# Four-layer hybrid decoder step on one core: contiguous cache sums, a shift added in PSUM, and layer sums kept in DRAM

## The chip, the core and the metric
The kernel runs on one NeuronCore of a Trainium2 chip. The core has five engines that each work through a list of instructions of their own, in order: TensorE (PE) multiplies matrices into PSUM; VectorE (DVE), ScalarE (ACT) and GpSimd (POOL) do elementwise work; SyncE (SP) issues most of the DMA transfers, and GpSimd issues the gathers. An engine that waits for a semaphore holds up everything behind it in its list. The metric is the device time of one execution in microseconds.

## The reference, cut to what matters
A trunk of four layers (short gated convolution, sparse attention, RG-LRU, short gated convolution) runs over 1024 prompt tokens and 32 sample tokens, with 1024 features. Every layer ends with an out-projection and a layer norm of the sum with its input. The attention of the sample tokens reads a paged cache; of its key and value rows, weighted sums over blocks of 32 are made.

```python
def layer_norm(x, g, b):
    xf = x.astype(jnp.float32)
    mu = jnp.mean(xf, axis=-1, keepdims=True)
    var = jnp.mean(jnp.square(xf - mu), axis=-1, keepdims=True)
    return ((xf - mu) * lax.rsqrt(var + LN_EPS) * g.astype(jnp.float32) + b.astype(jnp.float32)).astype(x.dtype)
...
past = cache_nsa_kv[j][page_table].reshape(bs, n_pages * PAGE_SIZE, 4, N_KV, HEAD_DIM)
...
blocks = full[:, :n_cmp * CMP_BLOCK, :2].reshape(bsz, n_cmp, CMP_BLOCK, 2, N_KV, HEAD_DIM)
kv_c = jnp.einsum('bnjcgd,cjgd->bncgd', blocks, w_cmp)
...
return (jax.nn.silu(z) * b_gate * conv) @ w_out, new_buf     # a mixer's end: the out-projection
...
yp = layer_norm(ALPHA * yp + mp, ln_g[i], ln_b[i])
ys = layer_norm(ALPHA * ys + ms, ln_g[i], ln_b[i])
```

## The kernel before
**Layout.** Activations lie transposed: X is eight tiles of 128 features by 1056 tokens. Tokens are cut into three blocks j of 352. So that fp32 matrices can be multiplied in three passes of the faster fp32r type, every operand is held as two halves, a rounded high part and the rest (`split`: ScalarE writes the rounded copy, VectorE or GpSimd subtracts). One output tile of 128 features by 352 tokens is 24 products (8 feature tiles x 3 pairs of halves), accumulated in one PSUM bank; `dense` and `dense_steps` issue them.

**Order.** The first layer, parts of the attention's projections, the third and fourth layers and all out-projections are recorded and then ordered by a planner (`Rec`). It simulates the engines with the prices of `cost`, gives buffers out of rings, and at every moment starts on each engine the ready step with the earliest due number. The order that comes out is fixed; on the chip the engines only wait for each other. The prompt attention between them has a plan of its own with prices of its own.

**Layer A with the cache sums.** While layer A runs its 96 output tiles, `compress` is advanced by 0.7 steps per tile (`share`, RATE). Its 64 steps (8 groups jg of rows x 8 samples b) each gather 1 MB of cache pages into a `big` buffer (GpSimd's indirect DMA), write half of it back to DRAM (`raw`), multiply the other half (4 x 256 columns) by the weights, on VectorE for even b and on GpSimd for odd, and reduce the four rows to 256 columns on VectorE. From the second group on, GpSimd adds this to the running sum. The ring of `big` buffers also holds X and layer A's results U, so the gathers have fewer buffers the further layer A is.

**An out-projection (`out_phase`).** It is run after layers 1 to 3 (ln 0, 1, 2), in row blocks c of 128 features: c = 0 to 3 for all three j, then c = 4 to 7 for j = 0, for j = 1, for j = 2. Each (c, j) makes y = ALPHA x + projection. For ln 0, x is put together from X's halves on GpSimd; for ln 1 and 2 it is read from DRAM. From row block 0, a product with a matrix of ones gives a shift per token (`kt`); the shift is subtracted from every later y on GpSimd, and the result and its square are summed over c in `ss`, on VectorE or GpSimd by the table `SUMS`. The shifted y is split into X's two halves in place, but for the last two or three row blocks, which stay in a `ws` buffer (`late`). After c = 7 of a block j, `norm(j)` takes statistics by products with ones, computes some twenty small operations, broadcasts scale and offset by further products, and for each c puts the halves together again on GpSimd, multiplies, adds, applies gain and bias on ScalarE, writes the result to DRAM and splits it into X for the next layer.

The last layer ends in another function (`final_phase`), which the change does not touch. In ln 1 four of the output tiles are made by the attention and come in as `done`.

Of the kernel before, what the change touches and what calls it, by code (L numbers as in the profile page):

```python
# [13 lines left out]
ALU = mybir.AluOpType  # L14
# [226 lines left out]
class Rec:  # L241
# [27 lines left out]
    def cost(self, eng, name, a, k, out):  # L269
# [226 lines left out]
class Trunk:  # L496
# [16 lines left out]
    def setup(self):  # L513
# [4 lines left out]
        self.dp = self.pool("scratch", 1, space=DRAM)  # L518
        self.pre = {}
# [5 lines left out]
        self.ones_m = self.cp.tile([P, P], F32, name="ones_m")  # L525
        nc.vector.memset(self.ones_m, 1.0 / D)

# [100 lines left out]
    def dense_steps(self, ps, w, X, sl):  # L628
        n = 0
        for k in range(NCH):  # L630
            xh, xl = X[k][:, 0, sl], X[k][:, 1, sl]
            for a, b in ((w[:, 0, k], xh), (w[:, 0, k], xl), (w[:, 1, k], xh)):
                self.nc.tensor.matmul(ps, a, b, start=n == 0, stop=n == 23)  # L633
                n += 1
# [42 lines left out]
    def out_phase(self, pm, wsrc, U, X, ln, lp, res=None, done={}, spill=None, final=None, nxt=()):  # L677


        nc = self.nc  # L680
# [3 lines left out]
        kt = self.wx.tile([P, 1088], F32)[:, 0:T]  # L684
# [12 lines left out]
        def norm(j):  # L697
# [34 lines left out]
            for c in range(NCH):  # L732
                self.rec.shift = AHEAD[self.later]["norm"]
                d = late[c][:, sl] if c in late else self.ct(TC)
                xh, xl = X[c][:, 0, sl], X[c][:, 1, sl]
                if c not in late:
                    nc.gpsimd.tensor_add(d, xh.bitcast(F32), xl.bitcast(F32))
                    nc.vector.tensor_mul(d, d, RB[0])
                    (nc.gpsimd if c in NADD[ln][j] else nc.vector).tensor_add(d, d, RB[1])
                else:  # L740
                    nc.vector.tensor_mul(d, d, RB[0])
                    (nc.gpsimd if c in NADD[ln][j] else nc.vector).tensor_add(d, d, RB[1])
# [14 lines left out]
        for c, j in order:  # L757
# [3 lines left out]
            if (c, j) not in done:  # L761
                ps = self.mm(pm)[:, 0:TC]
                self.dense(ps, W[c], U, j)
            if j == 2 and c >= 4:
                self.fetch(nxt[c - 4:c - 3])
# [3 lines left out]
            xh, xl = X[c][:, 0, sl], X[c][:, 1, sl]  # L769
            x = self.ct(TC)  # L770
            if (c, j) not in done:
                if res is None:
                    nc.gpsimd.tensor_add(x, xh.bitcast(F32), xl.bitcast(F32))
                else:
                    nc.sync.dma_start(x, res[c][:, sl], rk=[("x", ln - 1, c, j)])
                stt(out=y, in0=x, scalar=ALPHA, in1=ps, op0=ALU.mult, op1=ALU.add)
            d = y
# [1635 lines left out]
```

## Time and profile before

| what | value |
|---|---|
| median of 3 runs | 2470.85 us (2468.2 to 2470.94) |
| profiled execution, its own time | 2474.15 us |
| its span from first to last instruction | 2472.4 us |
| mean granted TensorE clock | 0.967 |
| TensorE busy | 2326.4 us, 94% |
| VectorE busy | 1688.7 us, 68% |
| ScalarE busy | 1225.4 us, 50% |
| GpSimd busy | 1149.1 us, 46% |
| moved by DMA | 303 MB, 123 GB/s mean |

The stages by time: the X tiles are loaded and transposed until some 40 us; layer A with the cache sums runs to about 420 us; the out-projection ln 0 follows, then the attention's projections and the sample tokens' attention to about 930 us, the prompt attention to about 1470, ln 1 to about 1600, the RG-LRU layer to about 1840, ln 2 to about 1970, and the last layer to the end. A busy TensorE is not TensorE at its peak: products are pipelined, and a stretch at the low clock counts as busy too. So stretches are compared by the number of products in them as well as by the busy time. Since one helper records all planned operations, nearly all have line 307; tiles and shapes tell them apart.

### The profile page before, as it was taken

What the parts mean: (1) busy time and instruction counts of PE and PEld (TensorE: products, weight loads), DVE (VectorE), ACT (ScalarE), POOL (GpSimd) and SP (SyncE); (2) the same over time, 40 slices, a digit from 0 to 9 for tenths busy, and PEclk for the clock granted to TensorE, in tenths of its full rate; (3) what the DMA queues carried; (4) which work ended last, traced back from release to release, by engine and by line L of the source; (5) the groups of instructions that cost most, each with busy time, mean ns of one, the idle gap of its engine ahead of it and who ended that gap; (6) DMA issues with size and microseconds to landing.
All of it is one profiled execution on the core that took longest, in us unless ns stands there. A gap on an engine that the chain in (4) does not pass through costs nothing. (4 is left out here: it accounts for less than half of the span.)

```text
span 2472.4 us, 41243 instructions
## 1 busy us (share of the span) xinstructions
PE 2326.4 (94%) x14740; PEld 2252.1 (91%) x14740; DVE 1688.7 (68%) x3588; ACT 1225.4 (50%) x2809; POOL 1149.1 (46%) x1261
## 2 busy tenths in 40 slices
PE   8999899888989989999999999889999899999997
PEld 8999899877878879999999988889999899999996
DVE  5867776688358777777777777888877863334336
ACT  3111111234448778888888873467974342122123
POOL 3555575766137755565565554633464640000122
PEclk9999999988999989999999999989999899999998
DMA  8999998425456752111111323221112121211111
GB/s 278 327 296 336 280 295 274 129 84 204 125 173 224 243 195 56 35 46 43 44 50 46 97 91 98 71 81 52 56 48 78 39 59 45 59 35 46 49 45 71
DMA packets 320816, 303.01 MB, mean 123 GB/s; under 512 B 17926, under 2 KB 287718, under 8 KB 311140
## 3 DMA queue, kind: packets, MB, share of 16 engines
q1 hardware_dynamic: 311396, 233.28, 30.7%
q0 software_dynamic: 9216, 67.11, 7.8%
q8 instruction: 116, 1.90, 0.3%
q14 instruction: 88, 0.72, 0.1%
HBM read 228.66 MB, written 75.83 MB: 123 GB/s over the span
## 5 line engine op out<-in xcount | busy, mean ns | idle before, releaser
L307 PE MATMUL mm<-x,w 128*128 128x352 f32 x5760 | 955.3, 327 | 31.2 <-DVE c L307 14.6
L307 PEld LDWEIGHTS mm<-x,w 128*128 128x128 f32 x5760 | 943.2, 192 | 38.2 <-DVE c L307 16.7
L307 PE MATMUL mm<-big,w 128*128 128x352 f32 x2208 | 386.3, 334 | 9.1 <-DVE c L307 3.9
L307 PEld LDWEIGHTS mm<-big,w 128*128 128x128 f32 x2208 | 371.2, 196 | 12.6 <-DVE c L307 4.5
L307 POOL TENSOR_TENSOR w<-ws,w 128x1024 fp32r<-128x1024 f32 (+1 forms) x43 | 105.3, 2449 | 400.2 <-ACT w L307 378.6
L1959 DVE TENSOR_TENSOR c<-T,c 128x512 fp32r<-128x512 f32 (+1 forms) x320 | 204.8, 648 | 49.2 <-ACT c L1955 44.5
L1955 ACT CAST c<-T 128x512 fp32r<-128x512 f32 (+1 forms) x320 | 174.6, 552 | 57.9 <-PE T L1951 38.0
L307 ACT CAST w<-ws 128x1024 fp32r<-128x1024 f32 (+2 forms) x116 | 120.6, 1039 | 163.8 <-PE mm L307 123.2
L633 PE MATMUL D<-x,w 128*128 128x352 f32 x1008 | 195.4, 330 | 2.1 <-DVE big L2086 2.0
L1861 PE MATMUL A<-big 128*128 128x320 f32 (+11 forms) x832 | 182.2, 335 | 3.4 <-DVE ast L1886 1.6
L1966 PE MATMUL O<-c,big 128*128 128x256 f32 x1056 | 180.2, 291 | 0.5 <-ACT c L1955 0.2
L307 ACT CAST big<-aux 128x352 fp32r<-128x352 f32 (+3 forms) x116 | 45.2, 402 | 243.6 <-DVE aux L307 165.5
L633 PEld LDWEIGHTS D<-x,w 128*128 128x128 f32 x1008 | 159.9, 188 | 5.6 <-DVE big L2086 3.5
L307 DVE TENSOR_TENSOR w<-ws,w 128x1024 fp32r<-128x1024 f32 (+2 forms) x73 | 91.6, 1255 | 99.7 <-ACT w L307 98.9
L1966 PEld LDWEIGHTS O<-c,big 128*128 128x128 f32 x1056 | 147.0, 189 | 2.5 <-DVE c L1959 0.7
L1919 POOL TENSOR_SCALAR pr<-pr,G,ast 128x32 f32<-128x32 f32 (+6 forms) x192 | 126.4, 674 | 47.1 <-DVE ast L1930 42.3
L1861 PEld LDWEIGHTS A<-big 128*128 128x128 f32 x832 | 134.8, 193 | 10.2 <-PE A L1861 2.2
L307 DVE TENSOR_REDUCE csum<-big 128x256 f32<-128x1024 f32 x56 | 111.5, 1992 | 40.9 <-POOL big L307 40.6
L1915 ACT ACTIVATE pr<-pr,ast 128x32 f32<-128x32 f32 (+6 forms) x192 | 118.4, 619 | 18.1 <-DVE ast L1886 17.0
L307 ACT ACTIVATE aux<-ws,PT 128x352 f32<-128x352 f32 (+2 forms) x72 | 42.8, 594 | 163.8 <-DVE ws L307 161.8
L307 DVE SCALAR_TENSOR_TENSOR c<-c,mm 128x352 f32<-128x352 f32 x143 | 72.9, 514 | 73.2 <-ACT c L307 49.0
L307 POOL TENSOR_TENSOR big<-big,ws 128x1024 f32<-128x1024 f32 (+1 forms) x40 | 87.9, 2198 | 68.6 <-DMA ws<-in_b_w_cmp 49.7
(287 smaller groups left out, 4364.7 us busy)
## 6 DMA issues: line engine op xcount, KB each, us to landing
ws<-in_a_w_in SPq DMA_DIRECT2D x64, 512.0 KB
raw<-big SPq DMA_DIRECT2D x128, 256.0 KB
big<-raw SPq DMA_DIRECT2D x128, 256.0 KB
xs<-x SPq DMA_DIRECT2D x24, 352.0 KB
x<-xs SPq DMA_DIRECT2D x8, 1056.0 KB
ws<-in_a_w_out SPq DMA_DIRECT2D x16, 512.0 KB
ws<-in_c_w_in SPq DMA_DIRECT2D x16, 512.0 KB
big<-ud SPq DMA_DIRECT2D x21, 352.0 KB
```

The source lines that it names most:

```text
L307: getattr(real, name)(*[f(x) for x in a], **{q: f(x) for q, x in k.items()})
L633: self.nc.tensor.matmul(ps, a, b, start=n == 0, stop=n == 23)
L1861: nc.tensor.matmul(o, q[:, hl, i * P:(i + 1) * P], k, start=m == 0, stop=m == 1)
L1915: nc.scalar.activation(S[:, a:a + m], S[:, a:a + m], AF.Exp, bias=st[:, k:k + 1], scale=-1.0, accum_out=st[:, 3 + k:4 + k])
L1919: nc.gpsimd.tensor_scalar(S[:, a:a + m], S[:, a:a + m], G[:, i, 16 * k + h:16 * k + h + 1], st[:, 6 + k:7 + k], op0=ALU.mult, op1=ALU.mult)
L1955: nc.scalar.copy(x["H"][:, 0:n], x["tp"][:, 0:n])
L1959: nc.vector.tensor_sub(x["L"][:, 0:n], x["tp"][:, 0:n], x["H"][:, 0:n].bitcast(F32))
L1966: nc.tensor.matmul(O, v, M[:, y * P:(y + 2) * P], start=done[0] == 0, stop=done[0] == total - 1)
```

## The change
**Cache sums.** The reduction over four strided rows becomes three contiguous additions on VectorE in place in the gathered buffer: rows 0 and 1 plus rows 2 and 3 (512 columns), then the two halves of that (256), then that onto the running sum (256). GpSimd's addition and the buffer `csum` are gone.

**Out-projections.** The shift is no longer subtracted from y: a 25th product, of the ones matrix with the scaled negative shift, is added in PSUM for every row block but the first. For this the ones and `kt` are fp32r. For ln 0, x is no longer put together: two VectorE operations add the two halves of X to the PSUM tile, one after the other. The shifted sums are no longer split into X; they go whole to a DRAM scratch `dd` and are read back in `norm`, so GpSimd's addition of the halves there is gone as well. The late row blocks stay in their buffers as before. The read-back has a due number 3 later than the rest of the norm (`DAHEAD`).

**Planner.** A product of 352 columns is now priced at 162 ns instead of 149, which moves steps in every planned part. The tables of due shifts and of engine choices are the same.

```diff
-            return max(free(m) / 2.4 * (4 if m.dtype == F32 else 1), 107) + 2
+            return max(free(m) / 2.27 * (4 if m.dtype == F32 else 1), 50) + 7
...
+        self.dd = self.dp.tile([NCH, P, T], F32, name="dd")
...
-        self.ones_m = self.cp.tile([P, P], F32, name="ones_m")
+        ones = self.cp.tile([P, P], F32R, name="ones_m")
+        self.ones_m = ones.bitcast(F32)
         nc.vector.memset(self.ones_m, 1.0 / D)
+        self.ones_r = ones
...
-    def dense(self, ps, w, X, j):
+    def dense(self, ps, w, X, j, extra=None):
-        for _ in self.dense_steps(ps, w, X, slice(j * TC, (j + 1) * TC)):
+        for _ in self.dense_steps(ps, w, X, slice(j * TC, (j + 1) * TC), extra is None):
             pass
+        if extra is not None:
+            self.nc.tensor.matmul(ps, self.ones_r, extra, start=False, stop=True)
...
                 xh, xl = X[c][:, 0, sl], X[c][:, 1, sl]
-                if c not in late:
-                    nc.gpsimd.tensor_add(d, xh.bitcast(F32), xl.bitcast(F32))
+                if c in late:
+                    d = late[c][:, sl]
+                else:
+                    d = self.ct(TC)
+                    self.rec.shift += DAHEAD
+                    nc.sync.dma_start(d, self.dd[c][:, sl], rk=[("d", ln, c, j)])
+                    self.rec.shift -= DAHEAD
...
             if (c, j) not in done:
+                ps = self.mm(pm)[:, 0:TC]
+                self.dense(ps, W[c], U, j, k if c else None)
                 if res is None:
-                    nc.gpsimd.tensor_add(x, xh.bitcast(F32), xl.bitcast(F32))
+                    stt(out=ps, in0=xl, scalar=ALPHA, in1=ps, op0=ALU.mult, op1=ALU.add)
+                    stt(out=y, in0=xh, scalar=ALPHA, in1=ps, op0=ALU.mult, op1=ALU.add)
...
-                nc.scalar.activation(kt[:, sl], kp, AF.Copy, scale=float(NCH))
-                d = ss[:, 0, sl]
-                nc.vector.tensor_sub(d, y, kt[:, sl])
+                nc.scalar.activation(k, kp, AF.Copy, scale=-8.0 * NCH)
+            d = ss[:, 0, sl] if c == 0 else y
+            if c == 0 or (c, j) in done:
+                stt(out=d, in0=k.bitcast(F32), scalar=0.125, in1=y, op0=ALU.mult, op1=ALU.add)
...
-                nc.gpsimd.tensor_sub(d, y, kt[:, sl])
...
             if c not in late:
-                self.split(xh, xl, d, "act", "dve")
+                nc.sync.dma_start(self.dd[c][:, sl], d, wk=[("d", ln, c, j)])
...
-                v = g4[:, :, 0:256].rearrange("p j f -> p f j")
-                o = acc[:, b]
+                o, v = acc[:, b], g4[:, :, 0:256]
+                nc.vector.tensor_add(v[:, 0:2], v[:, 0:2], v[:, 2:4])
                 if jg == 0:
-                    nc.vector.tensor_reduce(out=o, in_=v, axis=AX.X, op=ALU.add, wk=[("sum", n)])
+                    nc.vector.tensor_add(o, v[:, 0], v[:, 1], wk=[("sum", n)])
                 else:
-                    t = rt.tile([P, 256], F32)
-                    nc.vector.tensor_reduce(out=t, in_=v, axis=AX.X, op=ALU.add, wk=[("sum", n)])
-                    nc.gpsimd.tensor_add(o, o, t)
+                    nc.vector.tensor_add(v[:, 0], v[:, 0], v[:, 1])
+                    nc.vector.tensor_add(o, o, v[:, 0], wk=[("sum", n)])
...
+DAHEAD = -3
```

Three places show how the order moves. The first is VectorE at the end of layer A, where `csum<-big` (before) and `big<-big` (after) are the last cache sums, `c<-mm,c` and `aux<-c,aux` make layer A's last results, and `big<-aux,big` splits them into U. Before:

```order
L307 TENSOR_REDUCE csum<-big 128x256
L307 SCALAR_TENSOR_TENSOR c<-mm,c 128x352
L307 TENSOR_TENSOR aux<-c,aux 128x352
L307 SCALAR_TENSOR_TENSOR c<-mm,c 128x352
L307 TENSOR_TENSOR aux<-c,aux 128x320
L307 TENSOR_REDUCE csum<-big 128x256
L307 TENSOR_TENSOR big<-big,ws 128x4x256
L307 TENSOR_REDUCE csum<-big 128x256
L307 TENSOR_TENSOR big<-aux,big 128x352 x2
L307 TENSOR_TENSOR big<-aux,big 128x320
```

VectorE at the same place after:

```order
L307 TENSOR_TENSOR big<-big 128x2x256
L307 SCALAR_TENSOR_TENSOR c<-c,mm 128x352
L307 TENSOR_TENSOR big<-big 128x256 x2
L307 SCALAR_TENSOR_TENSOR c<-mm,c 128x352
L307 TENSOR_TENSOR aux<-c,aux 128x352
L307 TENSOR_TENSOR big<-aux,big 128x352
```

The last sums of the cache now stand ahead of the last three results, and each result's split follows it directly. The second place is GpSimd at the start of the out-projection ln 0, where `c<-x` puts X's halves together, `c<-c,ws` subtracts the shift and `big<-big,c` adds to `ss`. Before:

```order
L307 TENSOR_TENSOR big<-big,ws 128x4x256
L307 TENSOR_TENSOR c<-x 128x352
L307 TENSOR_TENSOR big<-big,csum 128x256
L307 TENSOR_TENSOR c<-x 128x352 x2
L307 TENSOR_TENSOR c<-c,ws 128x352
L307 TENSOR_TENSOR big<-big,c 128x352
```

GpSimd at the same place after:

```order
L312 DMA big<-in_cache_nsa_kv,idx_447 128x2048
L307 TENSOR_TENSOR big<-big,ws 128x4x256
L307 TENSOR_TENSOR w<-ws,w 128x1024
L307 TENSOR_TENSOR big<-big,c 128x352 x7
L307 TENSOR_TENSOR w<-ws,w 128x1024
```

Of the three kinds of additions only those into `ss` are left. The third place is TensorE at the end of ln 0, where `mm<-big` and `mm<-big,w` are the last output tiles, `mm<-w,x` and `mm<-big,x` of 384 columns are the next layer's, and `aux<-ones_m,big` are the statistics of the last block. Before:

```order
L307 MATMUL mm<-big 128x352 x18
L307 MATMUL mm<-w,x 128x384 x54
L307 MATMUL mm<-big,x 128x384 x6
L307 MATMUL aux<-ones_m,big 128x1 x6
L307 MATMUL mm<-big,x 128x384 x6
```

TensorE at the same place after:

```order
L307 MATMUL mm<-big 128x352 x24
L307 MATMUL mm<-ws,ones_m 128x352
L307 MATMUL mm<-w,x 128x384 x24
L307 MATMUL aux<-ones_m,big 128x1 x6
L307 MATMUL mm<-w,x 128x384 x12
```

The statistics stand after 24 products of the next layer instead of 60, and a product of `ones_m` closes the tile.

## Rows read from the trace of the kernel before

**Rows 1.** The page: busy time by engine, and clock by fortieth of the span.
```profile
PE 2326.4 (94%) x14740; PEld 2252.1 (91%) x14740; DVE 1688.7 (68%) x3588; ACT 1225.4 (50%) x2809; POOL 1149.1 (46%) x1261
...
PEclk9999999988999989999999999989999899999998
```

**Rows 2.** Stretches: busy us of PE, PEld, DVE, ACT, POOL; clock, DMA share, GB/s.
```profile
100.00:150.00 50.00, 50.00 (x313) 50.00 (x313) 32.17 (x37) 8.03 (x14) 28.78 (x21) 1.00 0.93 303
150.00:420.00 270.00, 250.74 (x1502) 248.19 (x1501) 207.12 (x227) 48.89 (x90) 164.55 (x115) 0.97 0.93 296
420.00:480.00 60.00, 47.73 (x269) 46.01 (x269) 40.06 (x46) 14.12 (x28) 38.75 (x32) 0.89 0.58 181
480.00:630.00 150.00, 125.30 (x662) 115.03 (x661) 113.41 (x171) 58.14 (x116) 94.55 (x86) 0.89 0.40 133
1520.00:1655.00 135.00, 115.63 (x640) 111.54 (x639) 115.67 (x223) 62.30 (x121) 70.59 (x62) 0.89 0.24 76
1920.00:2010.00 90.00, 78.25 (x444) 76.09 (x443) 76.90 (x138) 41.25 (x81) 55.71 (x50) 0.89 0.15 41
```

**Rows 3.** Timeline of PE in layer A: start, us, operation, count [idle before, releaser].
```profile
272.01 44.08 PE L307 MATMUL mm<-x,w 128*128 128x352 f32 x264 [5.12 <-DVE c L307]
...
443.95 1.88 PE L307 MATMUL aux<-idf,SC 128*18 128x128 f32 x8 [9.47 <-DVE big L307]
...
450.13 1.94 PE L307 MATMUL aux<-c,ones_m 128*128 128x352 f32 x6
```

**Rows 4.** Timeline of all engines, around 266 us and around 440 us.
```profile
266.27 5.27 DVE L307 COPY ws<-PT 128x16 f32<-128x16 f32 x1
...
266.86 2.35 POOL L307 TENSOR_TENSOR big<-big,ws 128x1024 f32<-128x1024 f32 x1
269.15 2.34 POOL L307 TENSOR_TENSOR w<-ws,w 128x1024 fp32r<-128x1024 f32 x1
...
437.34 1.88 DVE L307 TENSOR_REDUCE csum<-big 128x256 f32<-128x1024 f32 x1 [4.11 <-POOL big L307]
...
442.88 1.14 ACT L307 CAST big<-aux 128x352 fp32r<-128x352 f32 x3 [33.86 <-DVE csum L307]
```

**Rows 5.** Groups by shape, 100 to 450 us: busy us, mean ns | idle before.
```profile
L307 DVE TENSOR_REDUCE csum<-big 128x256 f32<-128x1024 f32 x54 | 107.6, 1992 | 40.9 <-POOL big L307 40.6
L307 DVE TENSOR_TENSOR big<-big,ws 128x1024 f32<-128x1024 f32 x27 | 47.1, 1745 | 35.6 <-DMA raw<-big 12.0 <-DMA ws<-in_a_w_in 10.4 <-DMA ws<-in_b_w_cmp 6.3
...
L307 POOL TENSOR_TENSOR big<-big,csum 128x256 f32<-128x256 f32 x54 | 54.7, 1012 | 74.0 <-DVE csum L307 72.4 <-DMA raw<-big 1.6
```

**Rows 6.** The same view, 2010 to 2400 us, where GpSimd is nearly idle.
```profile
L307 DVE TENSOR_TENSOR w<-ws,w 128x1024 fp32r<-128x1024 f32 x29 | 35.5, 1226 | 93.6 <-ACT w L307 93.1
```

**Rows 7.** The same view, 480 to 630 us, of VectorE, GpSimd and ScalarE.
```profile
L307 DVE TENSOR_TENSOR c<-c 128x352 f32<-128x352 f32 x29 | 24.6, 872 | 4.5 <-ACT c L307 3.7 <-POOL c L307 0.8
L307 DVE TENSOR_TENSOR x<-c,x 128x352 fp32r<-128x352 f32 x23 | 21.6, 952 | 5.0 <-ACT x L307 5.0
L307 DVE TENSOR_TENSOR big<-big,c 128x352 f32<-128x352 f32 x21 | 18.2, 886 | 6.3 <-POOL c L307 4.8 <-ACT c L307 1.6
...
L307 DVE SCALAR_TENSOR_TENSOR c<-c,mm 128x352 f32<-128x352 f32 x10 | 5.1, 511 | 0.4 <-POOL c L307 0.4
...
L307 POOL TENSOR_TENSOR c<-x 128x352 f32<-128x352 f32 x32 | 36.9, 1173 | 6.5 <-DVE big L307 3.6 <-PE aux L307 2.9
...
L307 ACT ACTIVATE c<-c 128x352 f32<-128x352 f32 x10 | 5.0, 496 | 20.4 <-POOL c L307 20.4
```

**Rows 8.** Timeline of VectorE around 572 us, in the norm of ln 0.
```profile
571.78 0.52 DVE L307 TENSOR_TENSOR c<-c 128x352 f32<-128x352 f32 x1
...
573.40 1.26 DVE L307 TENSOR_TENSOR c<-c 128x352 f32<-128x352 f32 x1
```

**Rows 9.** Waits of PE, 480 to 630 us: total us, times, longest.
```profile
PE aux L307 <- POOL big L307: 8.3, 2, 4.4
```

**Rows 10.** The chain that ended last, in order of time: start, us, what.
```profile
1888.62 2.20 DMA c<-xc
```

More of the change, by code (lines that the diff above doesn't have):

```diff
@@ L621, in load_w, with dense_steps @@
         return w
-    def dense(self, ps, w, X, j):
-        for _ in self.dense_steps(ps, w, X, slice(j * TC, (j + 1) * TC)):
-            pass
-    def dense_steps(self, ps, w, X, sl):
+    def dense(self, ps, w, X, j, extra=None):
+        for _ in self.dense_steps(ps, w, X, slice(j * TC, (j + 1) * TC), extra is None):
+            pass
+        if extra is not None:
+            self.nc.tensor.matmul(ps, self.ones_r, extra, start=False, stop=True)
+    def dense_steps(self, ps, w, X, sl, last=True):
         n = 0
@@ L632, in dense_steps @@
             for a, b in ((w[:, 0, k], xh), (w[:, 0, k], xl), (w[:, 1, k], xh)):
-                self.nc.tensor.matmul(ps, a, b, start=n == 0, stop=n == 23)
+                self.nc.tensor.matmul(ps, a, b, start=n == 0, stop=n == 23 and last)
                 n += 1
@@ L683, in out_phase @@
         ss = ss[:, 0:2 * T].rearrange("p (a n) -> p a n", a=2)
-        kt = self.wx.tile([P, 1088], F32)[:, 0:T]
+        kt = self.wx.tile([P, 1088], F32R)[:, 0:T]
         stat = lp.tile([P, 3, 24], F32, name="stat")
@@ L760, in out_phase @@
             sl = slice(j * TC, (j + 1) * TC)
[L761 to L765, printed above, removed]
+            xh, xl = X[c][:, 0, sl].bitcast(F32), X[c][:, 1, sl].bitcast(F32)
+            k = kt[:, sl]
             if j == 0 and NCH - c <= self.nws - 2 and c >= 4:
@@ L768, in out_phase @@
             y = done[c, j] if (c, j) in done else late[c][:, sl] if c in late else self.ct(TC)
-            xh, xl = X[c][:, 0, sl], X[c][:, 1, sl]
             x = self.ct(TC)
             if (c, j) not in done:
+                ps = self.mm(pm)[:, 0:TC]
+                self.dense(ps, W[c], U, j, k if c else None)
                 if res is None:
-                    nc.gpsimd.tensor_add(x, xh.bitcast(F32), xl.bitcast(F32))
+                    stt(out=ps, in0=xl, scalar=ALPHA, in1=ps, op0=ALU.mult, op1=ALU.add)
+                    stt(out=y, in0=xh, scalar=ALPHA, in1=ps, op0=ALU.mult, op1=ALU.add)
                 else:
                     nc.sync.dma_start(x, res[c][:, sl], rk=[("x", ln - 1, c, j)])
-                stt(out=y, in0=x, scalar=ALPHA, in1=ps, op0=ALU.mult, op1=ALU.add)
-            d = y
+                    stt(out=y, in0=x, scalar=ALPHA, in1=ps, op0=ALU.mult, op1=ALU.add)
+            if j == 2 and c >= 4:
+                self.fetch(nxt[c - 4:c - 3])
             if c == 0:
```

9 lines of the change are left out of this document (3 added, 6 removed).

## The prediction
> **What bounds the kernel now.** I read the page's first part and its clock line first, then a table of stretches, then the timeline and the groups of instructions inside the stretches where TensorE is not full. TensorE is busy for 94% of the span, and the clock line shows 9 or 8 tenths in nearly every slice [rows 1]: this is a kernel of one engine, and only what TensorE does, waits for, or does at the low clock counts. The stretch from 100 to 150 us shows it unhindered: 313 products of 352 columns in 50 us at clock 1.00, so 0.160 us for each [rows 2].
>
> In five stretches it is hindered. I call lost the idle time of PE plus (1 - granted clock) x stretch; the clock has two levels, 1.2 and 2.4 GHz, so a mean of 0.89 is some 22% of the stretch at the lower one, each time after a wait. By [rows 2]: layer A with the cache sums, 150 to 420, 270 - 250.7 + 0.03 x 270 = 27.4 us; its end, 420 to 480, 12.3 + 6.6 = 18.9; the first out-projection's norm and the next layer's start, 480 to 630, 24.7 + 16.5 = 41.2; the second out-projection, 1520 to 1655, 19.4 + 14.9 = 34.2; the third, 1920 to 2010, 11.8 + 9.9 = 21.7. Together 143 us. The change touches what runs in all five, and adds TensorE work; so the question is how much of the 143 comes back.
>
> **What ends the waits.** In layer A, PE waits 5.12 us before 272.0 and 9.47 us before 444.0, both for VectorE [rows 3]. The first is a VectorE copy of 16 columns that took 5.27 us: it lies over a GpSimd multiplication of 2.35 us and a GpSimd subtraction of 2.34 us that follow each other [rows 4]. The second is in-order blocking: VectorE stood 4.11 us at a cache reduction whose input GpSimd was still multiplying, and ScalarE's rounding of layer A's last U waited 33.9 us, up to 442.9, for such a reduction, because that U's buffer is one that a gathered page held [rows 4]. In the out-projections it is VectorE and GpSimd in step: beside GpSimd's additions a VectorE addition of 352 columns takes 1.26 us, without one 0.52 [rows 8]; over 480 to 630 these average 0.87 to 0.95 us, while the operation with one input in PSUM stays at 0.51 [rows 7].
>
> **The cache sums.** Removed for each of 64 gathered pages: a reduction of 1.992 us on VectorE and, for 56, an addition of 1.012 us on GpSimd with a round trip between the two engines [rows 5]. Added: VectorE additions of 512, 256 and (for 56 from memory to memory; the first eight end with the second) 256 columns. The trace has no such addition. Undisturbed, 1024 columns take 1.226 us [rows 6] and 352 take 0.52 [rows 8], so about 1.05 ns a column and 0.15 fixed: 0.69 + 0.42 + 0.42 = 1.53 us. Disturbed as the multiplications of the same stretch are (1.745 against 1.226, a factor of 1.42 [rows 5, 6]), 2.17 us. So VectorE changes by -0.46 to +0.18 us a page, -30 to +12 us in all, and GpSimd by -57 us. I take about -10 on VectorE, nearer the middle, since the partner that disturbs also gets lighter.
>
> What the trace shows here speaks against the change: the 54 reductions average 1.992 us while GpSimd is busy 61% of the time [rows 2, 5], close to each of them alone, and the multiplications beside them stretch. The Trainium skill says the same (SBUF — State Buffer, Who interferes with whom): a tensor_reduce never contends for the port pair shared with GpSimd, a tensor_tensor with both inputs in SBUF does when GpSimd reads SBUF. By that rule alone the 184 new additions are all exposed where 64 reductions were not; what this would do is the slower rival below.
>
> The instruction order gains more than the sums. The planner priced a PE product at 149 ns and now at 162, nearer to the 160 measured, and the last cache sums now stand before layer A's last convolution pieces on VectorE, not between them and their roundings. DMA is 93% busy here [rows 2], so late pages still stop VectorE. Of the 27.4 us I take 8 back (0 to 18), of the 18.9 at the end 13 (4 to 17: the 9.47 and its low clock).
>
> **The out-projections.** Added on PE: 61 products of ones with the shift (21, 19 and 21), in the same type as the others: 61 x 0.160 = 9.8 us, all on the path. The product that the kernel already makes with the plain fp32 ones takes 1.94 us for three [rows 3]; at that price it would be 39 us, which bounds it from above, but the operands' type is that of the 0.160 rows. The first product of this kind needs the shift of its block three groups earlier, 72 x 0.160 = 11.5 us; I cost that wait at nothing.
> GpSimd: 63 subtractions of the shift go (61 become the products, two become VectorE operations), and so do 72 additions that put X's halves together. At the 1.17 us that these take where it is worst [rows 7], that is up to 158 us less in three phases; in 480 to 630 GpSimd is busy 94.6 us [rows 2], 32 of its additions alone being 36.9 [rows 7]. VectorE: 48 subtractions of the split go, at 0.95 us [rows 7], -46; 24 PSUM operations come in layer A, 24 x 0.51 = +12; and what is left loses its partner: of the 73 additions and subtractions of 0.87 to 0.95 in 480 to 630 (the split among them) [rows 7] some 55 stay and fall toward 0.52, up to -20. ScalarE loses 48 roundings, -23 us, and no longer waits for GpSimd's subtraction (20.4 us before ten squares [rows 7]); that step lies in the chain from the last product to the statistics, for which PE waited 8.3 us on GpSimd [rows 9].
> Added on the queues: 48 writes and 48 reads of 176 KB. The DMA engines are 15 to 40% busy there [rows 2]. The nearest row for a read is that of the residual, 2.20 us on the chain [rows 10], against 1.17 for the GpSimd addition it replaces: between -1.2 (read ahead) and +1.0 us each, and only those of the last block of each phase can reach PE. Behind a write that waits for its sum on SP's queue stand the weight loads and the residual reads; the sums come every 4 us, so I cost it at nothing; if the cover is gone, one read's 2.2 us per phase.
> So the statistics come earlier and the norm of each block runs faster, but the chain of some twenty small operations stays, and the order now puts the last statistics product after 24 products of the next layer where 60 stood before, which uses up part of the gain. I take back 18 of 41.2 (6 to 32), 11 of 34.2 (2 to 24), 9 of 21.7 (0 to 16): under half each, the first most, since GpSimd falls most there.
>
> **Sum.** +9.8 - 8 - 13 - 18 - 11 - 9 = -49.2 us, against the profiled execution's 2474.15 (span 2472.4): 2425. The median of the runs is 3.3 us lower, 2470.85, so 2421.6, say 2422. With every bound at its worst, +9.8 - 12 = about 2469; at its best, +9.8 - 107 = about 2374.
>
> **The rivals.**
> A, larger: VectorE and GpSimd were the whole cause, and most of the lost time goes; 2374 to 2400. For: the two in step [rows 8]. Against: statistics and normalising are a chain of three engines, and DMA is still 93% busy in layer A.
> B, hidden: the freed engines are not the ones waited for; only the end of layer A is recovered. 2470.85 + 9.8 - 13 - (8 to 20 for all the rest) = 2448 to 2460. For: PE's named waits in 480 to 630 on VectorE and GpSimd are a part of the 41 only [rows 9]. If even the order's gain is eaten, 2466 to 2475: the change does nothing that counts.
> C, slower: the new additions are stopped by GpSimd in layer A. If each of the 184 loses what a multiplication loses, 1.745 - 1.226 = 0.52 us [rows 5, 6], a page of three costs 1.53 + 1.56 - 1.99 = +1.1 us, some 67 us more VectorE work in a stage with 63 us of idle VectorE in its longest stretch [rows 2]; VectorE becomes the bound there, PE's lost time doubles (+46) and its end is not recovered. 2471 + 10 + 46 - 38 = 2489. It decides from some 28 us more lost in layer A, where it outweighs the out-projections' 38 - 10. For: the 5.27 us copy [rows 4]. Against: GpSimd loses 57 us in that very stage, and its share of reading falls.
>
> **How the numbers follow.** The sum's own case, 2400 to 2447: 0.60. A: 0.13. B, 2447 to 2466: 0.13; nothing: 0.05. C: 0.09. The range takes in the sum's case, B and the upper half of A: 2385 to 2465. A measurement of this kernel can tell about 0.2%, 5 us, from no change: faster 0.86, same 0.05, slower 0.09.
>
> **What would show it.** In the profile after: TENSOR_REDUCE gone from VectorE, 512-column additions at 0.7 to 1.0 us and GpSimd 930 to 990 us busy instead of 1149; no wait over 5 us of PE between 420 and 450; 61 products that read ones_m at 0.16 us; VectorE's 352-column additions nearer 0.6 than 0.9 in the out-projections; no wait of VectorE over 1 us on a DMA from the scratch. I am wrong if PE's lost time in the out-projections stays above 80 us in sum, if the 256-column additions average over 0.8 us, or if VectorE stands at scratch reads.

## The result and the profile after

| what | before | after |
|---|---|---|
| median of the runs | 2470.89 us | 2443.03 us |
| range of the runs | 2468.2 to 2481.3 (4) | 2441.1 to 2450.3 (4) |
| profiled execution, its own time (span) | 2474.15 (2472.4) us | 2450.34 (2448.6) us |

The ratio is 0.9885 with a 95% interval of 0.985 to 0.992: faster by 28 us. I had forecast 2422, 49 us faster, in a range of 2385 to 2465. Sign and range hold; the likeliest value is 21 us off. The experiments show that this is no small miss: the two terms for the edits of the work were much too small, the instruction order had the wrong sign, and these errors partly cancelled.

The page of after, the busy times and the clock line, which answer to [rows 1]:

```profile
PE 2318.3 (95%) x14801; PEld 2247.7 (92%) x14801; DVE 1594.0 (65%) x3686; ACT 1206.7 (49%) x2761; POOL 955.4 (39%) x1070
...
PEclk9999998999999999999999999999989999999998
```

GpSimd lost 194 us (forecast: 930 to 990 busy; it is 955) and VectorE 95. TensorE has its 61 products more and still less time at the low clock: the mean granted clock is 0.971 after and 0.967 before. Where the gain is, and where it isn't, shows in stretches that hold the same TensorE work, within some 2%, as those of [rows 2] (columns as there):

```profile
150.00:426.00 276.00, 249.91 (x1502) 246.99 (x1500) 196.84 (x314) 48.30 (x89) 130.83 (x74) 0.96 0.93 308
426.00:477.00 51.00, 46.18 (x273) 44.69 (x274) 27.64 (x48) 12.92 (x22) 11.61 (x10) 0.91 0.31 96
477.00:604.00 127.00, 115.27 (x666) 107.20 (x664) 84.91 (x169) 53.14 (x100) 34.65 (x33) 0.96 0.58 194
1498.00:1616.00 118.00, 110.38 (x659) 107.84 (x657) 93.50 (x194) 55.97 (x111) 35.24 (x30) 0.94 0.39 123
1616.00:1900.00 284.00, 266.33 (x1611) 263.44 (x1611) 196.44 (x338) 184.42 (x306) 109.54 (x94) 0.97 0.21 63
1900.00:1983.00 83.00, 75.75 (x447) 75.14 (x446) 62.65 (x133) 40.42 (x78) 33.36 (x26) 0.90 0.25 78
```

Of the fifth there was no row in the prediction, since I did not look at that stage. Before, the RG-LRU layer read:

```profile
1655.00:1920.00 265.00, 260.97 (x1606) 258.50 (x1605) 202.50 (x351) 189.72 (x320) 121.53 (x106) 0.99 0.20 57
```

With "lost" as in the prediction (idle PE plus (1 - clock) x stretch), the terms of the sum come out so:

| term | lost before | lost after | change | forecast |
|---|---|---|---|---|
| layer A with the cache sums | 27.4 | 37.1 | +9.7 | -8 |
| its end | 18.9 | 9.4 | -9.5 | -13 |
| out-projection ln 0 | 41.2 | 16.8 | -24.4 | -18 |
| out-projection ln 1 | 34.2 | 14.7 | -19.5 | -11 |
| RG-LRU layer | 6.7 | 26.2 | +19.5 | 0 |
| out-projection ln 2 | 21.7 | 15.6 | -6.1 | -9 |
| 61 products of ones | | | +9.8 | +9.8 |

The sum is -20.5 against -23.8 of the two spans; the clock is given to two places, which is worth up to 5 us over these 940 us. So the out-projections gave more than forecast, layer A nothing in all, and the RG-LRU layer, whose instructions the diff does not touch, took 19.5 us.

### The profile page after: what moved, and what is told of

Its sections match the earlier page's. It is cut to its first block, busy times and chain, and to the rows that moved or that the text cites. A ratio compares the mean times of both kernels' runs of the same rounds, so it can differ in the third digit from the quotient of the medians.

```text
span 2448.6 us, 41435 instructions
## 1 busy us (share of the span) xinstructions
PE 2318.3 (95%) x14801; PEld 2247.7 (92%) x14801; DVE 1594.0 (65%) x3686; ACT 1206.7 (49%) x2761; POOL 955.4 (39%) x1070
## 5 line engine op out<-in xcount | busy, mean ns | idle before, releaser
L307 PEld LDWEIGHTS mm<-big,w 128*128 128x128 f32 x2208 | 366.3, 193 | 13.7 <-ACT c L307 6.9
L307 DVE TENSOR_TENSOR big<-big 128x256 f32<-128x256 f32 (+3 forms) x204 | 145.9, 730 | 39.0 <-POOL big L307 35.0
L307 DVE SCALAR_TENSOR_TENSOR c<-c,mm 128x352 f32<-128x352 f32 x125 | 64.3, 516 | 108.6 <-PE mm L307 53.9
```

Source lines behind the costliest of these rows:

```text
L307: getattr(real, name)(*[f(x) for x in a], **{q: f(x) for q, x in k.items()})
```

## Where to look: two waits in after

At 328 us PE waits 6.0 us for VectorE. The timeline of PE, VectorE and GpSimd there (start, us, engine, operation, idle before and what ended it):

```profile
328.06 40.82 PE L307 MATMUL mm<-x,w 128*128 128x352 f32 x240 [6.01 <-DVE c L307]
...
320.66 1.22 DVE L307 TENSOR_TENSOR big<-big,ws 128x1024 f32<-128x1024 f32 x1 [8.41 <-DMA ws<-in_b_w_cmp]
321.81 0.52 DVE L307 TENSOR_TENSOR big<-aux,big 128x352 fp32r<-128x352 f32 x1
322.24 5.33 DVE L307 TENSOR_TENSOR big<-big 128x512 f32<-128x512 f32 x3
327.49 0.52 DVE L307 SCALAR_TENSOR_TENSOR c<-mm,c 128x352 f32<-128x352 f32 x1
...
320.70 3.39 POOL L307 TENSOR_TENSOR big<-big,ws 128x1024 f32<-128x1024 f32 x1 [11.15 <-DMA ws<-in_b_w_cmp]
324.05 2.78 POOL L307 TENSOR_TENSOR w<-ws,w 128x1024 fp32r<-128x1024 f32 x1
```

VectorE stood 8.4 us until the weights of the cache sums had come, then did three cache additions, the first two held up by GpSimd (2.40 and 2.45 us), and only then, at 327.49, the operation that empties the PSUM bank for which PE stood. Nothing was wrong with that operation: it was queued behind work that was late.

At the end of layer A the last page is late in the same way:

```profile
423.67 2.81 DVE L307 TENSOR_TENSOR big<-big 128x512 f32<-128x512 f32 x1 [7.11 <-POOL big L307]
...
421.30 2.34 POOL L307 TENSOR_TENSOR big<-big,ws 128x1024 f32<-128x1024 f32 x1 [5.82 <-DMA big<-in_cache_nsa_kv,idx]
423.59 2.34 POOL L307 TENSOR_TENSOR w<-ws,w 128x1024 fp32r<-128x1024 f32 x1
...
429.80 1.02 PE L307 MATMUL aux<-idf,SC 128*18 128x128 f32 x4 [11.34 <-DVE big L307]
```

GpSimd waits 5.8 us for the page, VectorE 7.1 for GpSimd, and PE 11.3 for the results of layer A that stand behind. The 9.5 us wait of [rows 3], which I had said would go, is still there and longer.

## The experiments

**How stages are compared.** In each trace the columns that TensorE streams are summed up in order, the products of ones with the shift left out; that total is the same in all kernels. At equal sums, the time of the one trace less that of before tells how far a kernel is ahead (negative) or behind. The table gives what each stage adds, in us, for after and the twelve kernels of the experiments; an out-projection's figure contains its products of ones. The stage borders are at 460, 640, 1500, 1660, 1870 and 2020 us of before.

| kernel | price | layer A and its end | ln 0 | to the prompt attention's end | ln 1 | RG-LRU | ln 2 | rest |
|---|---|---|---|---|---|---|---|---|
| after | 162 | -3.6 | -20.0 | +1.0 | -16.5 | +17.2 | -4.0 | +1.8 |
| f_sums_out | 149 | -32.9 | -19.6 | +1.5 | -19.4 | -1.5 | -6.3 | -0.3 |
| f_out_price | 162 | +15.6 | -19.3 | -3.3 | -14.9 | +18.1 | -6.4 | +3.5 |
| f_price | 162 | +17.2 | -0.2 | +0.2 | +0.5 | +19.4 | +3.7 | +3.3 |
| g_price_first | 162, last part 149 | -10.7 | -20.2 | -1.7 | -18.7 | -1.1 | -4.8 | -0.4 |
| f_sums | 149 | -30.8 | +1.5 | -1.5 | -2.9 | -1.6 | -2.4 | 0.0 |
| h_rest_up | 162, others x 1.087 | -2.1 | -24.6 | +1.1 | -16.2 | +6.5 | -6.5 | -0.7 |
| h_true | 162, sums as measured | +6.0 | -16.8 | -2.8 | -16.1 | +15.4 | -14.4 | -0.3 |
| h_pe_low | 138 | -14.9 | -19.3 | -4.0 | -15.1 | +11.3 | -8.2 | -1.3 |
| d_raw_half | 162 | -33.2 | -19.9 | -4.0 | -16.2 | +19.3 | -4.0 | +1.8 |
| e_no_product | 149 | -34.0 | -14.7 | +1.3 | -10.0 | -1.1 | -3.6 | -0.4 |
| e_no_scratch | 149 | -28.4 | -13.6 | -0.6 | -9.8 | -1.1 | -3.5 | -0.3 |
| e_decode_low | 149, 138 in the middle | -26.3 | -18.8 | -2.1 | -19.4 | +0.1 | -5.8 | -0.4 |

Two pairs have one and the same order up to the end of ln 0: after and g_price_first (3.6 and 10.7 ahead), f_sums_out and e_decode_low (32.9 and 26.3). So layer A's column, where transfers decide, is good to some 7 us; the RG-LRU column repeats within 3. The table shows profiled executions: that of after is 7.3 us over the median of its runs, that of e_decode_low 9.9.

**The price taken back.** This kernel takes back the one edit that moves steps in stages which the rest does not touch. The line also gives short products another price, 109 ns instead of 57 for one column. The two stages that lose most, layer A and the RG-LRU layer, have none of these but eight transposes each, whose price of 109 stays.

```diff
-            return max(free(m) / 2.27 * (4 if m.dtype == F32 else 1), 50) + 7
+            return max(free(m) / 2.4 * (4 if m.dtype == F32 else 1), 107) + 2
```

> The changed kernel with the planner's old price of a TensorE product (149 ns for 352 columns) in all parts; sums and out-projections as changed. Stages are compared at equal TensorE work with the kernel before: after is 3.6 us ahead at the end of layer A, gains 20 in ln 0 and 17 in ln 1, then loses 19 in the RG-LRU layer (two waits of about 8 and 3 us and the low clock after them) and gains 6 in ln 2. Theory one, the price reorders the RG-LRU layer: here that layer costs 0 to 4 us instead of 19, and the whole is 2420 to 2435 if the end of layer A stays as it is, up to 2445 if the old order there costs some 10. Theory two, the out-projections' new shape (rings, read-backs, later weights) does it: the layer still loses 15 to 19, and the whole is 2440 to 2455.

Measured 2392.89 us (2392.5 to 2395.7), ratio to before 0.968 (0.966 to 0.971). Both theories had put it too high: the RG-LRU layer is back at before's time, as theory one said, and layer A, far from losing the new order's gain, wins 33 us. The stretch from 100 to 300 us of this kernel (columns as in [rows 2]):

```profile
100.00:300.00 200.00, 200.00 (x1246) 199.81 (x1246) 161.99 (x244) 39.40 (x70) 105.14 (x59) 1.00 0.99 329
```

TensorE does not stand for a moment there, beside DMA engines that are 99% busy. This is the version that beats both kernels.

**The price alone on the kernel before** (the same edit, the other way round).

> The kernel before with the planner's new price alone (162 ns). Theory one, the price reorders the RG-LRU layer for the worse: that stage loses 10 to 19 us against before and the whole is 2470 to 2490, less what the new order wins at the end of layer A (0 to 10). Theory two, the price matters only where it was meant to, at the end of layer A: RG-LRU within 3 us of before, the whole 2455 to 2471.

2514.75 us, ratio 1.017 (1.014 to 1.020): slower by 44 us, more than either theory. Layer A gives 17, RG-LRU 19. That settles the sign of the term that I had counted as a gain.

**The price in the first two parts only.** The planner gets a flag that is set ahead of the last part:

```diff
+            if self.old:
+                return max(free(m) / 2.4 * (4 if m.dtype == F32 else 1), 107) + 2
...
+        k.rec.old = True
```

> The changed kernel with the new price in the first two planned parts (to the sample tokens' attention) and the old one in the last part (ln 1, RG-LRU, ln 2, last layer). Up to the prompt attention it is the changed kernel. Theory one, the price reorders the RG-LRU layer: that layer costs 0 to 4 us against before instead of 19 and the whole is 2424 to 2432. Theory two, the out-projections' new shape does it: it still costs 15 to 19 and the whole is 2440 to 2446.

2415.32 us, ratio 0.978 (0.975 to 0.981), below the 2424 to 2432 expected, but theory one in its stage: RG-LRU -1.1 instead of +17.2, with ln 1 in its new shape ahead of it. The price does it, not the out-projections. The largest part of what the price does there stands in PE's timeline. After:

```profile
1811.67 11.73 PE L307 MATMUL mm<-x,w 128*128 128x352 f32 x72
1823.25 0.93 PE L307 MATMUL aux<-idf,SC 128*36 128x128 f32 x7
1831.97 0.40 PE L307 MATMUL aux<-idf,SC 128*36 128x128 f32 x1 [7.80 <-DVE SC L307]
```

The same place in f_sums_out, price 149:

```profile
1783.15 9.20 PE L307 MATMUL mm<-big,w 128*128 128x352 f32 x54
1792.19 0.75 PE L307 MATMUL aux<-c,ones_m 128*128 128x352 f32 x2
1792.78 0.49 PE L307 MATMUL aux<-idf,SC 128*36 128x128 f32 x3
1793.89 0.29 PE L307 MATMUL aux<-idf,SC 128*36 128x128 f32 x1 [0.62 <-DVE SC L307]
```

These transposes take states that VectorE's scans leave at the end of the layer. With 149 the plan puts 54 products of the next out-projection ahead of them, 9.2 us; with 162 they follow the layer's last products at once, and PE, which goes through its list in order, stands 7.8 us with those 54 products behind the waiting instruction. The wait is 7.8 in f_price too. The waits of PE in after, 1600 to 1850 us (total, times, longest):

```profile
PE aux L307 <- DVE SC L307: 7.8, 1, 7.8
PE mm L307 <- ACT c L307: 5.5, 5, 2.2
PE mm L307 <- DVE c L307: 2.9, 1, 2.9
```

At equal TensorE work, some 10 of the 17 us that after loses in this layer come at the transposes, where the granted clock is 0.77 from 1823 to 1845 us; the rest comes at the shorter waits before them. One reading: with TensorE dearer alone, everything else seems to finish earlier in TensorE's list than it does on the chip. Three kernels below test it.

**The sums as before, with the rest changed.** `compress` of before in the changed kernel:

```diff
-                nc.vector.tensor_add(v[:, 0:2], v[:, 0:2], v[:, 2:4])
...
+                    nc.vector.tensor_reduce(out=t, in_=v, axis=AX.X, op=ALU.add, wk=[("sum", n)])
+                    nc.gpsimd.tensor_add(o, o, t)
```

> The changed kernel with the cache sums as before (strided reduction on VectorE, running sum on GpSimd); out-projections and price as changed. Theory one, the new sums cost VectorE about as much as they save (three additions 1.045 + 0.559 + 0.559 = 2.16 us a page against 1.99) but free GpSimd, so that pages are asked for sooner and the DMA engines become the limit: without them layer A is 0 to 10 us slower than in the changed kernel and the whole is 2443 to 2455; GpSimd's waits for gathered pages are under 15 us where the changed kernel has 53. Theory two, the contiguous additions are slowed by GpSimd and are what holds layer A up after 300 us: without them layer A gains 8 to 15 us and the whole is 2428 to 2436.

2469.51 us, ratio 0.9995 (0.998 to 1.001): 26 us slower than after, more than theory one's 0 to 10 and against theory two. GpSimd waits 8 us for pages here and 78 for the reductions, as expected. Under the new price the out-projections alone gain nothing in all, since the price takes what they give.

**The sums alone, at the old price.**

> The kernel before with the new cache sums alone (old price of 149 ns, old out-projections). With the old price, sums and out-projections together are 32.9 us ahead of before at the end of layer A, and the out-projections alone (read under the new price) move that point by 1.6. If the sums are what makes layer A faster, this kernel is 25 to 33 us ahead there, nothing follows in ln 0 to ln 2 (within 3 us each), and the whole is 2437 to 2447. If contiguous additions are stopped by GpSimd's port (the slower rival of the prediction), layer A is behind before and the whole is 2475 to 2490. If only both together do it, 2455 to 2470.

2438.91 us, ratio 0.988 (0.985 to 0.992). Layer A is 30.8 us ahead and hardly anything follows, as the first branch said. With f_sums_out it shows that the parts add up: -30.8 for the sums, -45.3 for the three out-projections (19.6 + 19.4 + 6.3, products included).

How can the sums win 31 us, if VectorE's work for them does not shrink? Groups of after by shape, 100 to 450 us (busy us, mean ns | idle before), to set beside [rows 5]:

```profile
L307 POOL TENSOR_TENSOR big<-big,ws 128x1024 f32<-128x1024 f32 x27 | 71.2, 2636 | 97.8 <-DMA big<-in_cache_nsa_kv,idx 59.1 <-DMA ws<-in_b_w_cmp 38.5
L307 DVE TENSOR_TENSOR big<-big 128x256 f32<-128x256 f32 x109 | 60.1, 559 | 1.4
...
L307 DVE TENSOR_TENSOR big<-big 128x512 f32<-128x512 f32 x54 | 56.4, 1045 | 33.9 <-POOL big L307 32.7 <-DMA ws<-in_a_w_in 1.0
```

A page costs VectorE 1.045 + 2 x 0.559 = 2.16 us, my estimate of the disturbed case (2.17), against 1.99 for the reduction. What went is GpSimd's 54.7 us of running sums and the 72 us that GpSimd stood for the reductions [rows 5]; it now stands for the pages themselves. VectorE's other work beside it also got cheaper: the multiplication went from 1.745 to 1.612 us, and the copy that took 5.27 us in [rows 4] has a mean of 0.835 after against 1.427 before. PE's waits, 100 to 400 us, before:

```profile
PE mm L307 <- DVE c L307: 12.9, 6, 5.1
PE mm L307 <- DVE ws L307: 4.6, 2, 3.7
```

and in f_sums, where no other is left:

```profile
PE mm L307 <- DVE c L307: 1.7, 2, 1.1
```

So what went are PE's waits for VectorE and the low clock after them. Whether the shorter road through GpSimd does it, or the order that the planner makes of the other steps, no run here tells apart.

**Is it the ratio of prices?** If TensorE's price only has to stand right against the others', raising them all must bring the gain back; and if TensorE and the sums are both priced near what is measured, the plan should be at its best. Three kernels:

```diff
-        return self.record(eng, name, self.cost(eng, name, a, k, out), fn, outs, ins, out, rk, wk, a, k)
+        return self.record(eng, name, self.cost(eng, name, a, k, out) * (1 if eng == "PE" else 1.087), fn, outs, ins, out, rk, wk, a, k)
```

> The changed kernel, new price of 162 ns for a TensorE product, with the planner's prices of all operations of VectorE, ScalarE and GpSimd raised by the same ratio, 162/149 = 1.087. Theory one, what counts is the ratio of TensorE's price to the others' (with TensorE dearer alone, the plan sees idle VectorE time that the chip does not have, and puts side work ahead of what TensorE waits for): most of the 50 us come back, 2393 to 2412. Theory two, the tables of due shifts fit one set of prices only, and any other set loses: 2420 to 2460.

2434.01 us, ratio 0.985 (0.983 to 0.988): 9 of the 50 us come back, nearly all in the RG-LRU layer (+6.5 instead of +17.2), and even there the wait for the transposes stays (8.1 us). The time is in theory two's range.

```diff
+            if name in ("tensor_add", "tensor_mul", "tensor_sub") and not any(isinstance(v, View) and v.t.ring.tag in ("mm", "aux", "PT") for v in a):
+                return 1.4 * n + 200
...
-            return 2.1 * n + 150
+            return 2.4 * n + 180
```

> The changed kernel, new price of 162 ns, with additions and multiplications that read SBUF alone priced near what layer A measures: VectorE 1.4 ns a column + 200 (256 columns 559 ns, 512 1045, 1024 1612 measured; planned 337, 603, 1137), GpSimd 2.4 ns a column + 180 (1024 columns 2636 measured; planned 2300). Theory one, the loss comes from side work that is priced too low beside a TensorE price that is right: layer A comes back to 20 to 33 us ahead of before at its end, the RG-LRU layer by part, the whole 2390 to 2415. Theory two, the tables of due shifts fit one set of prices only: 2420 to 2470.

2449.05 us, ratio 0.992 (0.990 to 0.995): with these prices nearer to the measured means the plan is no better than after. The time is in theory two's range. The means are those of layer A, and each is a mix of operations that meet GpSimd's and of others that do not.

```diff
-            return max(free(m) / 2.27 * (4 if m.dtype == F32 else 1), 50) + 7
+            return max(free(m) / 2.59 * (4 if m.dtype == F32 else 1), 98) + 2
```

> The changed kernel with the price of a TensorE product further down, 138 ns for 352 columns. Theory one, the ratio: a TensorE that the plan takes for faster makes VectorE serve it first, so this is no slower than at 149: 2385 to 2400. Theory two, the tables of due shifts were made for 149, and a step to either side loses: 2405 to 2450.

2423.83 us, ratio 0.981 (0.979 to 0.984): a step of 11 ns to the other side loses 31 us as well. All three times lie in theory two's ranges, that the tables of due shifts go with one set of prices. That the tables are the reason is argued and not shown, since no run remakes them for another price. Nor does it say why each set loses: up to 410 us this kernel is as far ahead as f_sums_out (25.3 and 25.4), then it loses 18 at layer A's end and 11 in the RG-LRU layer, none of it at the transposes. Their place is a mechanism seen at one point; that one rule stands behind all of these losses is not shown.

**The order or the transfers?** In layer A the waits in after begin with late pages and late weights. This kernel keeps the order of TensorE, VectorE, ScalarE and GpSimd row for row and takes away transfers:

```diff
-                    nc.sync.dma_start(self.raw[b, :, jg, i], g4[:, :, 256 + P * i:384 + P * i])
+                    nc.sync.dma_start(self.raw[b, 0:P if i == 0 else 8, jg, i], g4[0:P if i == 0 else 8, :, 256 + P * i:384 + P * i]); self.rec.ops[-1].size = P * 4 * P * 4
```

> The changed kernel (price 162 ns) with the order of TensorE, VectorE, ScalarE and GpSimd kept row for row, but half of the raw page writes cut to 8 of 128 partitions (the selected values of the cache are then not written and the keys stand in their place, so the sample tokens' attention is wrong): some 16 MB less for the DMA engines in layer A, of 102 MB between 100 and 420 us. Theory one, at this order the late pages are what stops layer A: GpSimd's waits for gathered pages (53 us between 100 and 420 us) fall under 15, the point at the end of layer A goes from 3.6 us ahead of before to 12 to 33, and the whole is 2410 to 2434. Theory two, the order itself does it (VectorE stands at a late sum ahead of what TensorE needs, whatever the DMA does): the end of layer A stays within 5 us and the whole is 2436 to 2446.

2424.04 us, ratio 0.981 (0.979 to 0.984). Layer A is 33.2 us ahead, all that the old price gives: with some 16 of 102 MB less, the order of price 162 costs nothing there against f_sums_out, while RG-LRU, which has no such transfers, still loses 19. So the times are those of theory one. One number of it missed: GpSimd's waits for gathered pages stay at 56 us. What fell are the waits for the weights of the sums, which share SP's queue with the page writes. Waits in after, 100 to 420 us (total, times, longest):

```profile
POOL big L307 <- DMA big<-in_cache_nsa_kv,idx: 53.3, 16, 8.0
POOL big L307 <- DMA ws<-in_b_w_cmp: 38.5, 4, 12.0
DVE big L307 <- DMA ws<-in_b_w_cmp: 30.0, 4, 8.4
```

and in this kernel:

```profile
POOL big L307 <- DMA big<-in_cache_nsa_kv,idx: 56.2, 19, 5.1
...
POOL big L307 <- DMA ws<-in_b_w_cmp: 12.9, 2, 9.5
DVE big L307 <- DMA ws<-in_b_w_cmp: 11.1, 3, 5.2
```

Yet in f_sums_out GpSimd and VectorE wait 35.7 and 19.7 us for the same weights, and its PE does not stand from 100 to 400 us. So in layer A a late transfer cost time where the step that PE needs was queued behind the step that waits; order and transfers act together, and a change of either takes the loss away. The same cut of the writes at the old price was not run.

**Which edit of the out-projections?** Both on f_sums_out. First the shift goes back to GpSimd:

```diff
-                self.dense(ps, W[c], U, j, k if c else None)
+                self.dense(ps, W[c], U, j)
...
+            (nc.gpsimd if c else nc.vector).tensor_sub(d, y, k)
```

> The changed kernel with the old price (2392.9), but the shift is subtracted on GpSimd again instead of being added as a product of ones; scratch and PSUM additions of X stay. It saves TensorE 61 products, 9.8 us. Theory one, GpSimd's subtraction in the chain from the last product to the statistics is what the out-projections lost: ln 0, ln 1 and ln 2 give back more than the 9.8, each stage 5 to 12 us slower, the whole 2400 to 2425. Theory two, the gain is that of the scratch (no split, no putting together): the stages keep their 20, 19 and 8 us and gain the products' time, the whole 2380 to 2392.

2415.16 us, ratio 0.977 (0.975 to 0.980): 22 us slower than f_sums_out, although TensorE has 9.8 us less to do: theory one's whole, its stages 4.9, 9.4 and 2.7 us slower where 5 to 12 were expected. The chain that theory one named is back, in ScalarE's square that waits for GpSimd's subtraction (440 to 600 us), as in [rows 7], where it stood 20.4 us:

```profile
L307 ACT ACTIVATE c<-c 128x352 f32<-128x352 f32 x11 | 5.5, 500 | 18.5 <-POOL c L307 18.5
```

Then the scratch goes, and the split and GpSimd's additions come back:

```diff
-                nc.sync.dma_start(self.dd[c][:, sl], d, wk=[("d", ln, c, j)])
+                self.split(X[c][:, 0, sl], X[c][:, 1, sl], d, "act", "dve")
...
-                    nc.sync.dma_start(d, self.dd[c][:, sl], rk=[("d", ln, c, j)])
+                    nc.gpsimd.tensor_add(d, xh.bitcast(F32), xl.bitcast(F32))
```

> The changed kernel with the old price (2392.9), but the sums are split into X again (ScalarE and VectorE) and put together by GpSimd in the norm, without the scratch in DRAM; the products of ones and the PSUM additions of X stay. Theory one (the product is the gain): ln 0, ln 1 and ln 2 lose 0 to 4 us each, the whole 2390 to 2404. Theory two (the scratch is the gain): they lose 5 to 15 each, the whole 2410 to 2435. Both edits count when this kernel and the one without the products each lose.

2416.14 us, ratio 0.978 (0.975 to 0.981): the stages lose 6.0, 9.6 and 2.8 us, within theory two's 5 to 15 but for the last. Both edits count, by both tests. In the three stages the products win 17 us net of their own cost, the scratch 18; the other 10 of the 45 show in neither test. The two PSUM additions of X, which were not tried apart, may hold a part of them.

**Another price in the middle part.**

> The changed kernel with the old price (149 ns) in the first and last planned parts and 138 ns in the part of the sample tokens' attention, which gained 5.0 us from 640 to 930 us of before with 138 and lost 1.1 with 149. Theory one, the parts add up: 2386 to 2391. Theory two, that gain hung on what stood ahead of it: 2391 to 2400.

2391.64 us (2390.3 to 2401.5), ratio 0.967 (0.965 to 0.969): no difference from f_sums_out that its spread would show. The time lies where the two theories meet, so it decides neither. From 640 to 1500 us of before it gains 2.1, where f_sums_out lost 1.5 and h_pe_low gained 4.0: a part of that gain stays.

## Why the prediction was right, and where it was wrong

**Right in sign and range, and near by cancellation.** Against f_sums_out, the edits of the work gave 78 us, 28 more than the whole forecast, and the price took 50; the miss of 21 is the difference of the two. Without the price the time is that of rival A, 2374 to 2400. What bounds the kernel (TensorE's waits and the low clock after them), the places, and that both GpSimd and VectorE were in the way hold.

The rival "slower" fails at its price: it took 0.52 us for each of 184 additions. Over all 64 + 120 of them in after, those beside no GpSimd arithmetic take 0.685 and 0.421 us, the estimate of 0.69 and 0.42; only 12 and 9 lie beside it for over half of their time, and take 2.31 and 2.10. That is 12 x 1.62 + 9 x 1.68 = 35 us in all, 0.19 an addition, and brings VectorE's total for the sums to 129 us, against 64 x 1.992 = 127 of the reductions.

The rule of the Trainium skill (SBUF — State Buffer, Who interferes with whom) that speaks against the change, that additions from two SBUF inputs contend with GpSimd's reads and reductions do not, agrees with these additions, and with ten reductions before that lay beside GpSimd's arithmetic and took 2.02 us against 1.99 for those that lay beside none. It did not decide, because the partner is seldom there: GpSimd's arithmetic from 100 to 450 us fell from 155 to 101 us, and 21 of 184 additions met it. The 67 us of more VectorE work that the prediction gave this rival come out as 63 from its own terms. The prediction also says that the trace has no such addition. It has two VectorE operations of 512 columns with both inputs in SBUF, at 2430 and 2449 us, which took 0.685 us, close to the estimate of 0.69:

```profile
L307 DVE TENSOR_TENSOR big<-big 128x512 f32<-128x512 f32 x2 | 1.4, 685 | 0.0
```

**The step that failed: "the instruction order gains more than the sums".** I argued that a product priced at 162 ns, nearer to the 160 measured, gives a better order, and read the last cache sums' new place on VectorE as a gain. The price costs some 22 us in layer A (mean of the pairs of equal order: 29.6 ahead at 149, 7.2 at 162) and 17 to 19 in the RG-LRU layer. The medians say the same of the first two parts, 22 us from f_sums_out to g_price_first; the last part costs another 28, from there to after. Of the "-8" and "-13" for layer A and its end, the sums alone gave -31, and the price took most of it back: -3.6 in after. My two terms were too small for the sums and had no term for the loss.

**The stage left out.** The sum has no line for the RG-LRU layer, although the section on the change says that the price moves steps in every planned part. It took 17 to 19 us more in after, in a stage that lost 6.7 before. The place of the SC transposes could be seen in the order of the changed kernel before any run: 54 products ahead of them, and then none. What I had noted for the statistics of ln 0 (24 products ahead where 60 stood) is the same move, and I priced it there as using up "part of the gain" instead of looking for it elsewhere.

**Mis-sized: the out-projections.** Forecast -38 + 9.8 = -28, measured -40.5 in after and -45.3 at the old price. I took under half of what was lost because DMA and the chain of small operations stay; the lost time fell from 97 to 47. The signs named came out nearly as said, for 475 to 615 us of after:

```profile
L307 DVE TENSOR_TENSOR c<-c 128x352 f32<-128x352 f32 x29 | 19.8, 714 | 0.0
L307 DVE TENSOR_TENSOR big<-big,c 128x352 f32<-128x352 f32 x21 | 12.4, 608 | 1.1 <-ACT c L307 0.6
...
L307 DVE TENSOR_TENSOR x<-c,x 128x352 fp32r<-128x352 f32 x12 | 8.4, 707 | 0.3 <-ACT x L307 0.3
...
L307 PE MATMUL mm<-ws,ones_m 128*128 128x352 f32 x15 | 4.9, 325 | 0.0
```

VectorE's additions and subtractions took between 0.87 and 0.95 us before [rows 7]; now they take between 0.61 and 0.71 and hardly wait; the products of ones last 325 ns, as their neighbours do (326 and 331 on the page; products overlap, so each adds half of that), and none in these three stretches waits for its shift. No wait of VectorE on the scratch appears; GpSimd and ScalarE have none on its reads either. The PE wait at layer A's end that was to go is 11.3 us.

**The signs that should have warned.** "Late pages still stop VectorE" stood in the prediction and was used only to shrink a gain. In after late transfers turn the new order into a loss; what fell with the loss in d_raw_half were the waits for the late weights, not those for the pages.

## What to carry to other kernels

A truer price did not make a better plan: with the tables of due shifts left as they were, some 8% on the price of one operation, to either side, cost 30 to 50 us on a kernel whose other edits gain 78. Judge an edit of prices or order apart from the edit of the work, and go through every stage that the order touches, not only those that the diff touches. When a freed engine gives back more or less than its busy time, look at what is queued in order behind its waits.

## What the runs showed that I had not expected

An addition of VectorE that meets GpSimd's arithmetic is not slowed by a factor; it ends when GpSimd's operation has ended, and a fixed time later: the one at 423.67 in the timeline above took 2.81 us beside a GpSimd operation of 2.34 and ended 0.55 us after it. So did all 17 cache additions of after that took over 1 us: those of 512 columns ended some 0.55 us after the GpSimd operation beside them, those of 256 columns some 0.28. Beside none they took 0.685 and 0.421. A mean of 1.045 us over the group of 512 columns is a mix of two kinds, and a factor taken from a mean (my 1.42) says nothing of a single instruction.

With DMA engines 99% busy at 329 GB/s for 200 us, TensorE stood for nothing; at 1.01 to 1.03 and 346 to 351 GB/s in after it was busy for 97.4 and 97.1 of 100 us, so it stood some 5 us in all. With the order of after and a share of 0.93 at 317 GB/s (d_raw_half) it stood for nothing again. So DMA engines near 99% did not by themselves stop TensorE; the place of the waiting steps did, where transfers came late.
